# Second output projection: which heads its early part covers, and on which queue their rows are read

## Chip, cores and metric

The kernel runs on one core of one Trainium2 chip. The metric is the device time of one execution in microseconds. Beside the times there is a profile of one execution: the instructions of each engine with their start and duration, the DMA transfers, and what each engine waited for.

Engines: TensorE (PE; its weight loads are listed apart as PEld), VectorE (DVE), ScalarE (ACT), GpSimd (POOL) and SyncE (SP, which here only issues DMAs). Each engine has a stream of instructions of its own, and a DMA issue is an instruction in the stream of the engine that issues it.

## What is computed

A trunk of two layers over 1024 tokens of width 1024. Layer 0 mixes tokens by windowed attention, layer 1 by a bidirectional gated linear recurrence (HGRN2) of eight heads. Each mixer also has four cross-attention heads into 256 memory tokens. All twelve heads of 128 columns share one output projection, and a ConvGLU block follows. The part that matters is layer 1's mixer and its output projection:

```python
def mixer_hgrn2(u, mem_kv, w_in, lb_fwd, lb_bwd, norm_g, w_out):
    q, i, zf, zb, gate, xq = jnp.split(u @ w_in, [...], axis=-1)
    ...
    o = (gla_chunked(q, k_f, v, lf_f)
         + flip_t(gla_chunked(flip_t(q), flip_t(k_b), flip_t(v), flip_t(lf_b))))
    o = rmsnorm(o, norm_g.reshape(HG_HEADS, HG_VAL_DIM)).reshape(bsz, t, HG_W).astype(u.dtype)
    o = o * jax.nn.silu(gate)
    return jnp.concatenate([o, memory_cross_attn(xq, mem_kv)], axis=-1) @ w_out

    # in the trunk
        h = h + rmsnorm(y, norm_g[layer, 1])
        f = conv_ffn(rmsnorm(h, norm_g[layer, 2]), ...)
        h = h + rmsnorm(f, norm_g[layer, 3])
```

## The kernel before

**Precision.** Large products are made of three matmuls. An operand x is split into `h` (ACT casts it to fp32r) and `l` (DVE subtracts `h` from x). `mm3` (L81 to L83) then adds up h·h, h·l and l·h. So each operand costs an ACT instruction and a DVE instruction before PE may use it, and each weight unit (L75 DMA into a staging tile `st`, L76 cast, L77 subtraction) as well.

**Layer 1's mixer** (`hgrn`). Heads 0 to 7 run one after another. The normalised input lies transposed in `uh` and `ul`, eight blocks of 128 rows by 1024 tokens. A head is projected from it (matmuls into `pj`), then goes through four passes (two directions by two halves of 512 tokens), a long chain of small DVE, ACT and PE steps (`E`, `EP`, `ER`, `pa`, `pt`, `kT`, `pu`, `S`). At the end of the head, `output` makes `po`, normalises it (`on`, L1304), transposes it (`pt`, L1308) and, for heads 0 to 6, scales it into `ot` (L1316) and stores it from SP to the DRAM tensor `oT[1]` (L1317), one store for each half of the tokens, the upper half first. Head 7 isn't stored: its result is split straight into block 7 of `uh` and `ul` (L1312, L1313), whose input columns nobody needs any more. The projections of head 7 are spread over its passes: the last two are f for the upper half of the tokens (f1) and b for the lower half (b0). The cross-attention heads are fitted between the passes of the even heads and store their rows into blocks 8 to 11 of `oT[1]` from ACT (L224).

**The second output projection** (class `Out`, object `wo1`). It contracts the twelve blocks with weights in six units; unit u serves heads 2u and 2u+1. The output's 1024 columns are made in two halves of 512. The eight token tiles of 128 go in the order 4, 5, 6, 7, 0, 1, 2, 3. `groups` names which heads are contracted when, in the first half of the columns:

- `begin` (early part): for each tile, `read` brings the rows of `groups[0]`, here heads 0 to 6, from `oT[1]` into the place of the used-up `ul` (L536, on SP) and splits them (L537 on ACT, L538 on DVE); `kept` multiplies them into a PSUM bank `pb` (3 matmuls for each head); L569 copies the bank to `y0`. Two banks, which the projections used until then, are taken in turn. PE can do this while head 7 is still in its passes.
- `finish` (late part): for each tile, `cross` reads and multiplies the cross heads 8 to 11 (L551, L86, L87), `kept` adds `groups[2]`, here head 7, and L598 adds the early part's `y0`. Four more PSUM banks come with it.
- then, still in `finish`, the second half of the columns: all of heads 0 to 7 from `uh` and `ul`, then the cross heads again, then the residual, the norm and its transposition back into `uh` and `ul` for the ConvGLU block.

**Weight units.** `units` is the order in which they are loaded: the first four go to a ring of four slots as head 7's projection weights leave it (L76 and L77 with `wh`, `wl`), the last two to a pool of their own (`xwh`, `xwl`) whose memory is free only when head 7's passes are done. Before, the order is 0, 1, 2, 3, 4, 5.

**What sets the order.** Nobody writes the streams out by hand. A scheduler, which runs the program against its own estimates of durations, puts each instruction into the stream of its engine when it is ready and free by those estimates; among those that are ready the one earlier in the program goes first, and `tc.high_priority(AHEAD)` moves an instruction 2000 places ahead in that ranking. On the chip the streams then stand fixed. Before, layer 1's reads have no such priority (`self.order[:2 - 2 * self.l]` is empty for l = 1).

`Out` serves layer 1 alone; layer 0's projection has a class of its own, which the change leaves as it is.

Of the kernel before, what the change touches and what calls it, by code (L numbers as in the profile page):

```python
# [6 lines left out]
F32 = mybir.dt.float32  # L7
# [9 lines left out]
P = 128  # L17
# [29 lines left out]
def build(tc, A, out):  # L47
    nc = tc.nc
    act, dve, pool, pe = nc.scalar, nc.vector, nc.gpsimd, nc.tensor
# [3 lines left out]
    oT = [dram.tile([12, P, T], F32, name=f"oT{l}") for l in range(2)]  # L53
# [15 lines left out]
    def wunit(src, n=1024, pl=None, eng=None):  # L69

        tg = ("wh", "wl") if pl is None else ("xwh", "xwl")
        h = (pl or ring).tile([P, 1024], F32R, tag=tg[0], name=tg[0])
        l = (pl or ring).tile([P, 1024], F32R, tag=tg[1], name=tg[1])
        raw = stg.tile([P, 1024], F32, tag="st", name="st")[:, :n]
        nc.sync.dma_start(raw, src)  # L75
        act.copy(h[:, :n], raw)  # L76
        (eng or dve).tensor_tensor(l[:, :n], raw, h[:, :n].bitcast(F32), op=ALU.subtract)  # L77
        return h, l
# [10 lines left out]
    def rstd_of(pl, ss, n, count, tag):  # L89
        ms = pl.tile([P, n], F32, tag=tag + "ms", name=tag + "ms")  # L90
        dve.tensor_scalar(ms, ss, 1.0 / count, EPS, op0=ALU.mult, op1=ALU.add)
        rs = pl.tile([P, n], F32, tag=tag + "rs", name=tag + "rs")
        pool.tensor_tensor(rs, ms, nhalf[:, :n], op=ALU.pow)
        return rs

    def sumsq(pl, src, ss, j=None):
        n = src.shape[-1]
        if j is None:
            j = pl.tile([P, n], BF16, tag="junk", bufs=1, name="junk")
        act.activation(j[:, :n], src, AF.Square, accum_out=ss)  # L100

    def grow(pl, src_row, name):
        g = pl.tile([P, D], F32, tag=name, bufs=1, name=name)
        nc.sync.dma_start(g, src_row.to_broadcast([P, D]))
        return g
# [265 lines left out]
    class WOut:  # L371
# [3 lines left out]
        def __init__(self, l, src, key, order):  # L375
            self.l, self.src, self.key, self.order = l, src, key, order
            self.pools = [[], [], []]
            self.pre, self.part, self.begun, self.us = {}, {}, {}, {}
            self.psb, self.tag, self.psb2 = None, "pb", None
# [29 lines left out]
        def bank(self):  # L409
            if self.psb2:  # L410
                return self.psb2.tile([P, 512], F32, tag="pb2", name="pb")
            return self.psb.tile([P, 512], F32, tag=self.tag, name="pb")
# [99 lines left out]
    class Out:  # L512

        def __init__(self, l, src, key, order):
            self.l, self.src, self.key, self.order = l, src, key, order
            self.us, self.wf, self.banks, self.used = {}, None, [], 0
            n = (6, 7)[l]
            self.groups = (range(0, n), range(8, 12), range(n, 8))
            self.units = ((0, 1, 2, 4, 5, 3), (0, 1, 2, 3, 4, 5))[l]

        def bank(self):
            pl, tag = self.banks[self.used % len(self.banks)]
            self.used += 1
            return pl.tile([P, 512], F32, tag=tag, name="pb")

        def load(self, b, pl=None, n=6):
            for i, u in enumerate(self.units[:n]):
# [1 line left out]
                    self.us[b, u] = wunit(A[self.key][b, u], pl=pl if i >= RING else None)  # L529
            self.b = b  # L530

        def read(self, t):
            k = self.groups[0]
            c = (slice(None), slice(0, len(k)), slice(t * P, (t + 1) * P))
            raw = ul[c].bitcast(F32)
            nc.sync.dma_start(raw, oT[self.l][0:len(k), :, c[2]].rearrange("k p t -> p k t"))  # L536
            act.copy(uh[c], raw)  # L537
            dve.tensor_tensor(ul[c], raw, uh[c].bitcast(F32), op=ALU.subtract)  # L538

# [15 lines left out]
                c = slice((k % 2) * 512, (k % 2 + 1) * 512)  # L555
                mm3(ps, oh[:, i, :], ol[:, i, :], wh[:, c], wl[:, c], first and i == 0, last and i == 3)

        def begin(self, psb, tag, n, y0):
            self.psb, self.y0 = psb, y0
            self.banks += [(psb, tag)] * n  # L560
            for t in self.order:
                if t in self.order[:2 - 2 * self.l]:
                    with tc.high_priority(AHEAD):
                        self.read(t)
                else:
                    self.read(t)
                ps = self.bank()
                self.kept(ps, t, self.groups[0], True, True)
                act.copy(y0[t], ps)  # L569
            self.used = 0  # L570
# [11 lines left out]
        def finish(self):  # L582
            l = self.l
            self.wf = tc.alloc_tile_pool(name=f"wf{l}", bufs=1, side="right", reuse_waits="tile") if l == 0 else None
            wp = tc.alloc_tile_pool(name=f"wo{l}", bufs=2, side="right", reuse_waits="tile")
            psp = tc.alloc_tile_pool(name=f"wops{l}", bufs=2, space=PSUM, side="right", reuse_waits="tile")
            n = NT - 2 - len(self.banks)
            psb2 = tc.alloc_tile_pool(name=f"wopc{l}", bufs=n, space=PSUM, reuse_waits="tile")
            self.banks += [(psb2, "pb2")] * n
            y0 = self.y0  # L590
            s0 = wp.tile([P, NT], F32, bufs=1, name="s0")
            for t in self.order:
                ps = self.bank()
                self.cross(ps, t, True, False)
                self.kept(ps, t, self.groups[2], False, True)
                if t == self.order[5]:
                    after = self.last_read
                dve.tensor_tensor(y0[t], ps, y0[t], op=ALU.add)  # L598
                sumsq(wp, y0[t], s0[:, t:t + 1])
            with tc.issue_after(after.ins):  # L600
                g1 = grow(wp, A["norm_g"][l, 1:2, :], "g1")
                g2 = grow(wp, A["norm_g"][l, 2:3, :], "g2")
                xs = {}
                for t in self.order[:2]:
                    xs[t] = self.rows(wp, t)
            self.load(1, self.w1)
            self.first = wunit(A["ffw1"][l, 0, :, :1024], pl=self.wf) if l == 0 else None
            for t in self.order:
                pool.tensor_tensor(y0[t], y0[t], g1[:, :512], op=ALU.mult)
            for t in self.order:  # L610
                ts_ = slice(t * P, (t + 1) * P)
                ps = self.bank()
                self.kept(ps, t, range(8), True, False)
                self.cross(ps, t, False, True)
                x = xs[t] if t in xs else self.rows(wp, t)
                ss = wp.tile([P, 1], F32, tag="ss1", name="ss1")
                sumsq(wp, ps, ss)
                y1 = wp.tile([P, 512], F32, tag="y1", name="y1")
                dve.tensor_tensor(y1, ps, g1[:, 512:], op=ALU.mult)
                dve.tensor_tensor(ss, ss, s0[:, t:t + 1], op=ALU.add)  # L620
                rs = rstd_of(wp, ss, 1, D, "p")
                for c, y in ((slice(0, 512), y0[t]), (slice(512, 1024), y1)):
                    dve.scalar_tensor_tensor(x[:, c], y, rs[:, 0:1], x[:, c], op0=ALU.mult, op1=ALU.add)
                nc.sync.dma_start(h1d[l][ts_, :], x)
                norm_T(wp, psp, x, g2, uh, ul, t)
            psp.release()
            psb2.release()
            self.psb.release()
            wp.release()
            self.w1.release()  # L630
# [412 lines left out]
    def hgrn():  # L1043
        l = 1
# [7 lines left out]
        psj = tc.alloc_tile_pool(name="hgpj", bufs=2, space=PSUM, reuse_waits="tile")  # L1052
        PB = dict(pt=2, pu=1, po=1)

        def bank(tag, shape=(P, 4, P)):
            return psp.tile(list(shape), F32, tag=tag, bufs=PB[tag], name=tag)

        class Bank:
            tile = staticmethod(lambda shape, dt, tag, bufs, name: psp.tile(shape, dt, tag=tag, bufs=bufs, name=name))

        tags = {"pj": ("pj", 2, psj), "ps": ("pt", 2, Bank), "pt": ("pt", 2, Bank), "po": [lambda x=x: bank(x, (P, 512)) for x in ("po", "pu")], "sm": 1, "xo": "ot"}
        one = lambda shape, name, dt=F32: wp.tile(shape, dt, bufs=1, name=name)
        for x in PB:
            bank(x)
# [292 lines left out]
            if h < 7:  # L1357
                cur = proj(h + 1)
        free = [x[:, i].rearrange("p a b -> p (a b)") for i in (2, 0) for x in (V, G)]
        wo1.begin(psj, "pj", 2, {t: free[i // 2][:, (i % 2) * 512:(i % 2 + 1) * 512] for i, t in enumerate(wo1.order)})  # L1360
        psp.release()
        wp.release()
        return late
# [32 lines left out]
    wo1 = Out(1, h2d, "wout1", [4, 5, 6, 7, 0, 1, 2, 3])  # L1396
    start()
    window()
    wo0.finish()
    ffn(0, wo0, h2d, True, (0, 1), (0, 1))  # L1400
    late = hgrn()
    wo1.finish()
    late.release()
# [84 lines left out]
```

## Time and profile before

| | |
|---|---|
| time, median of 3 runs | 2695.96 us (2693.84 to 2696.16) |
| the profiled execution | 2697.36 us, of which the span is 2695.5 us |
| PE, PEld busy | 2622.5 us (97%), 2202.1 us (82%) |
| DVE, ACT, POOL busy | 1831.1 us (68%), 1385.1 us (51%), 468.2 us (17%) |
| early part: first split on ACT, last copy to `y0` | 1896.2 us, 1950.2 us |
| late part: first cross matmul | 1949.7 us |
| early reads L536, 8 of 448 KB | issued 1892.3 to 1903.1 us, 5.5 us to landing (median) |
| cross reads L551, 12 of 256 KB from 1880 to 1980 us | issued 1913.4 to 1976.4 us |

How to read it: times are microseconds from the start of the span. A line of the timeline is the start, the duration, engine, source line, operation, output<-inputs by the program's names, and in brackets how long the engine had idled before it and what it waited for. A line of the waits is "who <- whom: us in total, times, longest". The chain is followed back from the last instruction, at each step to what released it. The granted clock (PEclk) is TensorE's, as a share of full speed.

### The profile page before, as it was taken

The page shows a single profiled execution, that of the slowest core. Times are in us where ns is not written, and L with a number is a line of the kernel's source. Part 1 is how long each engine was busy: PE and PEld are TensorE (multiplying, and loading weights), DVE is VectorE, ACT ScalarE, POOL GpSimd, SP SyncE. Part 2 cuts the span into 40 slices and gives each one's busy share as a digit, 9 for nine tenths or more (in the row PEclk, how much of TensorE's full clock was granted, in tenths as well). Part 3 has the DMA queues.
Part 4 walks back from the last instruction along what each step waited for, and adds up shares of the span by engine and source line. Part 5 has one row for each costly group of instructions (what it writes and reads, how often), then busy time and mean ns, then how long its engine had stood idle before and what let it go on. Part 6 is the DMA issues. An engine that isn't in the chain of part 4 may idle for free.

```text
span 2695.5 us, 39322 instructions
## 1 busy us (share of the span) xinstructions
PE 2622.5 (97%) x14496; PEld 2202.1 (82%) x14496; DVE 1831.1 (68%) x3024; ACT 1385.1 (51%) x2528; POOL 468.2 (17%) x520
## 2 busy tenths in 40 slices
PE   8899999999999999999999999999899999999998
PEld 7888897788888887887887888888788788888887
DVE  6487777678655555478778686886657756556447
ACT  6367666645444445454455554555534444444443
POOL 1221110111111100032223141231121111110013
PEclk9899999999999999999999999999999999999999
DMA  7674213557877756574225252101446777775656
GB/s 281 209 163 108 59 28 115 178 181 181 217 196 203 200 168 244 190 243 149 102 98 160 77 128 60 48 29 63 120 166 164 198 198 205 197 203 159 224 193 233
DMA packets 205362, 427.00 MB, mean 158 GB/s; under 512 B 20080, under 2 KB 67568, under 8 KB 199536
## 3 DMA queue, kind: packets, MB, share of 16 engines
q1 hardware_dynamic: 178176, 329.83, 37.5%
q0 software_dynamic: 24544, 90.19, 16.1%
q10 hardware_dynamic: 2448, 4.46, 0.4%
q8 instruction: 114, 1.87, 0.3%
q14 instruction: 80, 0.66, 0.1%
HBM read 331.08 MB, written 117.44 MB: 166 GB/s over the span
## 4 chain that ended last, share of the span: by engine, by line
PE 76%; DVE 13%; ACT 4%; DMA 4%; issue 2%; POOL 1%; SPq 0%; DVEq 0%; POOLq 0%; ACTq 0%
PE X L639 26%; PE V L639 11%; PE pj L81 5%; PE pj L82 5%; PE Y L639 5%; PE pj L83 5%; PE pb L82 3%; PE pb L81 3%; PE pb L83 3%; DVE E L1195 1%; DVE ER L1230 1%; DVE wl L77 1%; PE pt L338 1%; DVE wl L87 1%; PE pt L116 1%
## 5 line engine op out<-in xcount | busy, mean ns | idle before, releaser
L87 DVE TENSOR_TENSOR wl<-st,wh 128x1024 fp32r<-128x1024 f32 (+1 forms) x238 | 263.5, 1114 | 324.7 <-ACT wh L86 303.1
L86 ACT CAST wh<-st 128x1024 fp32r<-128x1024 f32 (+1 forms) x238 | 222.5, 936 | 288.9 <-PE X L639 191.4
L81 PE MATMUL pj<-uh,wh 128*128 128x512 f32 x512 | 204.1, 399 | 4.9 <-DVE xl L87 2.5
L639 PE MATMUL X<-wl,wh 128*128 128x512 f32 x528 | 204.8, 390 | 0.3 <-DVE wl L87 0.3
L639 PE MATMUL X<-wh,wl 128*128 128x512 f32 x528 | 204.6, 389 | 0.0
L82 PE MATMUL pj<-ul,wh 128*128 128x512 f32 x512 | 202.8, 396 | 0.1
L83 PE MATMUL pj<-uh,wl 128*128 128x512 f32 x512 | 202.2, 395 | 0.0
L639 PE MATMUL X<-wh 128*128 128x512 f32 x528 | 198.8, 390 | 0.8 <-ACT c L1012 0.6
L81 PE MATMUL pj<-wh,uh 128*128 128x384 f32 (+1 forms) x512 | 191.0, 373 | 3.9 <-DVE gs L1126 3.9
L82 PE MATMUL pj<-wl,uh 128*128 128x384 f32 (+1 forms) x512 | 187.9, 367 | 0.0
L83 PE MATMUL pj<-wh,ul 128*128 128x384 f32 (+1 forms) x512 | 187.4, 367 | 0.0
L77 DVE TENSOR_TENSOR wl<-st,wh 128x1024 fp32r<-128x1024 f32 (+1 forms) x92 | 121.6, 1328 | 29.1 <-ACT wh L76 28.1
L639 PE MATMUL V<-uh,wh 128*128 128x512 f32 x344 | 133.8, 389 | 0.0
L639 PE MATMUL V<-ul,wh 128*128 128x512 f32 x344 | 133.8, 389 | 0.0
L639 PE MATMUL V<-uh,wl 128*128 128x512 f32 x344 | 133.8, 389 | 0.0
L76 ACT CAST wh<-st 128x1024 fp32r<-128x1024 f32 (+1 forms) x99 | 99.9, 1015 | 52.3 <-PE pj L82 30.2
L81 PEld LDWEIGHTS pj<-uh,wh 128*128 128x128 f32 x512 | 97.1, 190 | 25.4 <-DVE xl L87 2.9
L639 PEld LDWEIGHTS X<-wh 128*128 128x128 f32 x528 | 99.1, 188 | 22.2 <-ACT c L1012 1.0
L639 PEld LDWEIGHTS X<-wl,wh 128*128 128x128 f32 x528 | 99.1, 188 | 21.1 <-DVE wl L87 0.7
L639 PEld LDWEIGHTS X<-wh,wl 128*128 128x128 f32 x528 | 99.1, 188 | 20.5
L83 PEld LDWEIGHTS pj<-uh,wl 128*128 128x128 f32 x512 | 97.0, 189 | 19.2
L82 PEld LDWEIGHTS pj<-ul,wh 128*128 128x128 f32 x512 | 96.9, 189 | 18.8 <-DVE ul L87 0.4
(366 smaller groups left out, 7204.9 us busy)
## 6 DMA issues: line engine op xcount, KB each, us to landing
st<-hid SPq DMA_DIRECT2D x154, 256.0 KB, 3.1
st<-in_ffw_dram SPq DMA_DIRECT2D x108, 256.0 KB, 3.2
w2s<-in_ffw_dram POOLq DMA_DIRECT2D x24, 1024.0 KB, 7.8
st<-in_ffw_dram SPq DMA_DIRECT2D x46, 512.0 KB, 3.8
hid<-tt SPq DMA_DIRECT2D x88, 256.0 KB, 4.6
st<-w2s SPq DMA_DIRECT2D x88, 256.0 KB, 3.1
sx<-in_ffw_dram SPq DMA_DIRECT2D x84, 256.0 KB, 4.0
sy<-in_ffw_dram SPq DMA_DIRECT2D x42, 512.0 KB, 6.2
```

What stands on the lines that cost most here:

```text
L76: act.copy(h[:, :n], raw)
L77: (eng or dve).tensor_tensor(l[:, :n], raw, h[:, :n].bitcast(F32), op=ALU.subtract)
L81: pe.matmul(o, ah, bh, start=first, stop=False)
L82: pe.matmul(o, ah, bl, start=False, stop=False)
L83: pe.matmul(o, al, bh, start=False, stop=last)
L86: act.copy(h, src)
L87: dve.tensor_tensor(l, src, h.bitcast(F32), op=ALU.subtract)
L116: pe.transpose(ps[:, k, :], u[:, (4 * b + k) * P:(4 * b + k + 1) * P], ident)
L338: pe.transpose(tp[:, j, :], sm[:, j, c * P:(c + 1) * P], ident)
L639: pe.matmul(o, x, y, start=new, stop=e, skip_group_check=not first)
L1195: dve.tensor_tensor_scan(B[:, rev], smask, a_[:, rev], 0.0, op0=ALU.mult, op1=ALU.add)
L1230: dve.tensor_tensor(re_, re_, bc(pl_[:, :, e:e + 1], [P, nb, n]), op=ALU.mult)
```

## The change

The early part takes heads 0 to 5, and the late part heads 6 and 7. The early rows are read from ACT's queue instead of SP's; the reads and splits of the first two tiles (4 and 5) get the priority AHEAD. Head 6's rows are read apart, after the early part in the program, from SP's queue, in two transfers of 512 tokens, the upper half first. The load order of the weight units becomes 0, 1, 2, 4, 5, 3, so that the ring's fourth slot takes unit 4 (cross heads 8 and 9), and the separate pool takes units 5 and 3. The rewritten `bank` and `banks` name the number of buffers of each tag; for this kernel it stays two and four.

```diff
@@ class Out, __init__
-            n = (6, 7)[l]
-            self.groups = (range(0, n), range(8, 12), range(n, 8))
-            self.units = ((0, 1, 2, 4, 5, 3), (0, 1, 2, 3, 4, 5))[l]
+            self.groups = (range(0, 6), range(8, 12), range(6, 8))
+            self.units = (0, 1, 2, 4, 5, 3)
@@ bank
-            pl, tag = self.banks[self.used % len(self.banks)]
+            pl, tag, n = self.banks[self.used % len(self.banks)]
             self.used += 1
-            return pl.tile([P, 512], F32, tag=tag, name="pb")
+            return pl.tile([P, 512], F32, tag=tag, bufs=n, name="pb")
@@ read
-        def read(self, t):
-            k = self.groups[0]
-            c = (slice(None), slice(0, len(k)), slice(t * P, (t + 1) * P))
+        def read(self, ks, c0, c1, eng):
+            c = (slice(None), slice(ks[0], ks[-1] + 1), slice(c0, c1))
             raw = ul[c].bitcast(F32)
-            nc.sync.dma_start(raw, oT[self.l][0:len(k), :, c[2]].rearrange("k p t -> p k t"))
+            eng.dma_start(raw, oT[self.l][ks[0]:ks[-1] + 1, :, c0:c1].rearrange("k p t -> p k t"))
             act.copy(uh[c], raw)
             dve.tensor_tensor(ul[c], raw, uh[c].bitcast(F32), op=ALU.subtract)
@@ begin
-        def begin(self, psb, tag, n, y0):
+        def begin(self, psb, tags, y0):
             self.psb, self.y0 = psb, y0
-            self.banks += [(psb, tag)] * n
-            for t in self.order:
-                if t in self.order[:2 - 2 * self.l]:
+            self.banks += [(psb, t, tags.count(t)) for t in tags]
+            eng = (nc.sync, act)[self.l]
+            for i, t in enumerate(self.order):
+                if i < 2:
                     with tc.high_priority(AHEAD):
-                        self.read(t)
+                        self.read(self.groups[0], t * P, (t + 1) * P, eng)
                 else:
-                    self.read(t)
+                    self.read(self.groups[0], t * P, (t + 1) * P, eng)
@@ hgrn, its end
-        wo1.begin(psj, "pj", 2, {t: free[i // 2][...] for i, t in enumerate(wo1.order)})
+        wo1.begin(psj, ("pj",) * 2, {t: free[i // 2][...] for i, t in enumerate(wo1.order)})
+        for b in (1, 0):
+            wo1.read(range(6, 7), b * 512, (b + 1) * 512, nc.sync)
```

More of the change, by code (lines that the diff above doesn't have):

```diff
@@ L588, in finish @@
             psb2 = tc.alloc_tile_pool(name=f"wopc{l}", bufs=n, space=PSUM, reuse_waits="tile")
-            self.banks += [(psb2, "pb2")] * n
+            self.banks += [(psb2, "pb2", n)] * n
             y0 = self.y0
@@ L1359, in hgrn @@
         free = [x[:, i].rearrange("p a b -> p (a b)") for i in (2, 0) for x in (V, G)]
-        wo1.begin(psj, "pj", 2, {t: free[i // 2][:, (i % 2) * 512:(i % 2 + 1) * 512] for i, t in enumerate(wo1.order)})
+        wo1.begin(psj, ("pj",) * 2, {t: free[i // 2][:, (i % 2) * 512:(i % 2 + 1) * 512] for i, t in enumerate(wo1.order)})
+        for b in (1, 0):
+            wo1.read(range(6, 7), b * 512, (b + 1) * 512, nc.sync)
         psp.release()
```

## The prediction

> **What bounds the kernel now.** I read the page first, then the busy time of each engine in stretches around the change, the waits of TensorE there, and the chain that ended last.
>
> ```profile
> span 2695.5 us, 39322 instructions
> ...
> PE 2622.5 (97%) x14496; PEld 2202.1 (82%) x14496; DVE 1831.1 (68%) x3024; ACT 1385.1 (51%) x2528; POOL 468.2 (17%) x520
> ```
>
> TensorE (PE) has work in 97% of the span, so only a hole on PE can be won, and a hole filled early moves the end. The stretches:
>
> ```profile
> core 0: us, PE busy (x) PEld busy (x) DVE busy (x) ACT busy (x) POOL busy (x), PEclk, DMA share, GB/s
> 1883.60:1885.70 2.10, 2.04 (x69) 1.52 (x68) 2.10 (x6) 1.67 (x4) 0.65 (x3) 1.00 0.01 4
> 1885.70:1889.70 4.00, 0.00 (x0) 0.00 (x0) 3.97 (x6) 1.80 (x4) 1.01 (x1) 1.00 0.37 109
> 1889.70:1897.20 7.50, 3.58 (x16) 2.94 (x16) 6.15 (x14) 5.19 (x10) 1.53 (x2) 0.77 0.70 214
> 1897.20:1901.30 4.10, 4.08 (x73) 3.41 (x74) 4.09 (x7) 3.44 (x5) 1.01 (x2) 0.58 1.01 273
> 1901.30:1920.00 18.70, 18.37 (x152) 15.05 (x151) 17.62 (x29) 9.51 (x16) 5.83 (x6) 1.00 0.43 113
> 1920.00:1950.00 30.00, 30.00 (x162) 25.64 (x161) 13.03 (x25) 13.49 (x31) 4.17 (x4) 1.00 0.21 63
> ...
> 1977.00:2040.00 63.00, 63.00 (x300) 52.61 (x299) 38.71 (x64) 23.96 (x49) 9.65 (x14) 1.00 0.40 142
> ```
>
> Columns: the stretch, its length, then busy us of PE, weight loads, DVE, ACT, POOL, then the granted clock. From 1885.70 to 1901.30 PE idles 4.00 + 3.92 + 0.02 = 7.9 us. The last projection matmul of the eighth head (head 7):
>
> ```profile
> 1883.21 0.40 PE L83 MATMUL pj<-uh,wl 128*128 128x512 f32 x1
> ```
>
> The early part of the second output projection starts only at 1897.2. The waits in the hole, then the chain through it:
>
> ```profile
> PE pt L1269 <- ACT ot L1316: 4.1, 1, 4.1
> PE pb L81 <- ACT uh L537: 3.2, 1, 3.2
> ```
>
> ```profile
> 1889.08 0.60 ACT ot L1316
> 1889.69 2.55 DMA oT<-ot
> ...
> 1892.31 3.90 DMA ul<-oT
> 1896.23 0.95 ACT uh L537
> 1897.22 0.54 PE pb L81
> ```
>
> The early part reads heads 0 to 6 in one transfer, so it needs head 6 written: ACT makes `ot`, it lands 2.55 us later, only then is `ul` read (3.90), split (0.95), multiplied. Heads 0 to 5 had long been in DRAM.
>
> **The clock in the hole.** The rows give 0.77 and 0.58. At full clock the busy 3.58 and 4.08 us would have been 3.58 x 0.77 and 4.08 x 0.58, so 0.8 + 1.7 = 2.5 us are lost to it. The Trainium skill (TensorE: Matmul & The Clock Gate, "What's actually happening") says that an idle window of about 3.4 us halves the clock until about as long a busy one; one such window costs 1.7 us, an estimate from that page. The trace has a slow stretch of 11.6 us, longer than one such window, so the row stands; by the page the sum below would be 0.8 us smaller.
>
> The hole is thus worth 7.9 + 2.5 = **10.4 us** at most, plus 0.3 from 1901.30 to 1920.00 that I leave aside.
>
> **The change, part by part.**
>
> *Reads of heads 0 to 5 alone.* The wait for `ot` and its landing is gone. What remains is that the columns of `ul` and `uh` are free and the weights ready:
>
> ```profile
> 1874.84 0.68 DVE L1145 TENSOR_SCALAR s<-pj 128x512 f32<-128x512 f32 x1
> 1875.44 1.21 DVE L77 TENSOR_TENSOR wl<-st,wh 128x1024 fp32r<-128x1024 f32 x1
> ...
> 1885.15 0.69 DVE L1145 TENSOR_SCALAR s<-pj 128x512 f32<-128x512 f32 x1
> 1885.76 2.04 DVE L77 TENSOR_TENSOR wl<-st,wh 128x1024 fp32r<-128x1024 f32 x1
> ```
>
> The order of token tiles is 4, 5, 6, 7, then 0 to 3. Columns 512 and up (tiles 4 to 7) are last read by the projection that L1145 empties at 1874.84 (f1), columns below 512 by b0, emptied at 1885.15. The third weight unit, heads 4 and 5, is split by 1875.44 + 1.21 = 1876.65; only the fourth comes at 1887.8, and after the change that is the cross heads' unit, needed much later. So tiles 4 and 5 can be read from about 1875, land by 1879 (3.90) and be split before PE runs dry at 1885.7. PE then has two tiles at once, 2 x 18 matmuls. One matmul costs 0.228:
>
> ```profile
> 2050.18 5.48 PE X L639 x24
> ```
>
> so 36 x 0.228 = 8.2 us, and with the transposes and products of head 7 that ran in the hole (3.58 x 0.77 = 2.8) PE is fed to 1885.7 + 11.0 = 1896.7.
>
> *First two splits ahead.* They come before head 7's chain on ACT and DVE. The durations, grouped by shape:
>
> ```profile
> L538 DVE TENSOR_TENSOR ul<-ul,uh 128x896 fp32r<-128x896 f32 x8 | 8.9, 1116 | 1.8 <-ACT uh L537 1.8
> L537 ACT CAST uh<-ul 128x896 fp32r<-128x896 f32 x8 | 7.5, 942 | 4.5 <-DMA ul<-oT 4.4
> ...
> L87 DVE TENSOR_TENSOR ol<-ol,oh 128x512 fp32r<-128x512 f32 x5 | 3.3, 685 | 6.1 <-ACT oh L86 6.1
> ...
> L86 ACT CAST oh<-ol 128x512 fp32r<-128x512 f32 x5 | 3.1, 621 | 4.9 <-DMA ol<-oT 3.0 <-PE pb L82 1.9
> ```
>
> For 768 columns, between 512 and 896: DVE 0.685 + 2/3 x 0.431 = 0.97, ACT 0.84. All ten splits (eight of 768, two of 512) cost DVE 8 x 0.97 + 2 x 0.69 = 9.1 against 8.9, ACT 7.9 against 7.5: +0.2 and +0.4 us. Two pulled ahead put 1.9 us of DVE before head 7's chain.
>
> ```profile
> 1870.00:1921.00 51.00, 42.67 (x389) 35.24 (x388) 47.87 (x86) 29.86 (x56) 14.48 (x15) 0.93 0.40 114
> ```
>
> DVE is busy 47.87 of 51 us there and spares only 3.1; ACT spares 21.1. So DVE is full, and the third tile's split, which is not ahead, gets its turn late. Before, the first split found its place on DVE at 1897.2, after a gap that shows how the chain ahead of it ebbs:
>
> ```profile
> 1897.20 1.09 DVE L538 TENSOR_TENSOR ul<-ul,uh 128x896 fp32r<-128x896 f32 x1 [1.03 <-ACT uh L537]
> ```
>
> PE runs dry at 1896.7; with the subtraction after it that is a pause between 0 (splits squeezed in earlier) and 3 us. I take **1.5**.
>
> *ScalarE's queue.* Eight issues leave SP and go to ACT, in whose stream an instruction holds up all behind it. The bounds of one issue: the stores that ACT issues already, and SP's own issues of these rows:
>
> ```profile
> L224 ACTq DMA_DIRECT2D oT<-xo x16: 326/326/343, 213.4 to 1884.9; - x16
> ```
>
> ```profile
> 1892.31 3.23 SPq L536 DMA_DIRECT2D ul<-oT  x4
> ...
> 1901.46 3.50 SPq L536 DMA_DIRECT2D ul<-oT  x4
> ```
>
> So 8 x 0.33 = 2.6 us below, and (3.23 + 3.50) x 6/7 = 5.8 above. The second is the same access, so I take 5.8; ACT's 21.1 us of spare time hide it, unless it falls in head 7's exponentials that DVE waits for. Nothing for the sum, 0 to 2 for the range. In exchange SP's queue no longer holds reads behind stores:
>
> ```profile
> SPq L536 <- DMA oT<-ot: 6.6, 2, 4.4
> ```
>
> The Trainium skill (DMA: Bandwidth & Descriptors, "Issuing engines are not separate DMA queues") speaks against this part: another issuing engine saves its issue time, not transfer time. By that rule the queue alone would gain at most the 6.7 us of SP's issues, none of them on PE's path; what the row above shows is an ordering wait of 6.6 us on SP, and that is what goes.
>
> *Head 6's rows later.* Two reads of 256 KB on SP, after head 6's stores; behind them wait the cross heads' reads, of which the first goes out at 1913.4:
>
> ```profile
> L551 SPq DMA_DIRECT2D ol<-oT x12: 360/371/507, 1913.4 to 1976.4; - x12
> ```
>
> That is 12 us after the last of head 6's stores had landed (1901.46 in the row of SP above), so nothing is delayed. The 24 matmuls (8 x 3) of head 6 move to the late part, 24 x 0.228 = 5.5 us moved, not saved.
>
> *Order of weight units.* In the second half unit 3 is split last, as it was already:
>
> ```profile
> 1983.09 2.32 DVE L77 TENSOR_TENSOR wl<-st,wh 128x1024 fp32r<-128x1024 f32 x1
> ```
>
> It ends at 1985.4. PE does two tiles' first six heads, 36 matmuls or 8.2 us, before it needs it, and the second half begins near 1977:
>
> ```profile
> 1985.07 0.39 PE L83 MATMUL pb<-wh,ul 128*128 128x512 f32 x1
> ```
>
> So it is needed at 1985.1 to 1985.4. There is no slack, so a microsecond later is a microsecond lost; a microsecond earlier wins nothing. Its slot comes free at the same matmul as before. I take 0, -0 to +2.
>
> *The tail of head 7.* PE reaches the end of the early part sooner, by 10.4 and by the 5.5 moved:
>
> ```profile
> 1938.82 1.13 DVE L1304 SCALAR_TENSOR_TENSOR on<-po,ors,gs 128x128 f32<-128x128 f32 x4 [1.19 <-POOL ors L93]
> ...
> 1944.48 0.75 DVE L1313 SCALAR_TENSOR_TENSOR ul<-pt,bng,uh 128x512 fp32r<-128x512 f32 x1 [4.53 <-ACT uh L1312]
> ```
>
> ```profile
> 1949.71 0.62 PE L81 MATMUL pb<-xwh,oh 128*128 128x512 f32 x2
> ```
>
> Before, head 7's rows were ready at 1945.2, 4.5 us ahead of PE's first late matmul at 1949.7. After, PE is there at 1949.7 - 10.4 - 5.5 = 1933.8 and has the cross heads of two tiles without new banks (24 x 0.228 = 5.5, to 1939.3), of six with all banks (16.4, to 1950.2). Head 7's chain has slack too: its `on` was done at 1939.95 and its subtraction ended 5.3 us later, 4.5 of which DVE idled for a transpose whose turn on PE had not come and the copy behind it. Shortfall 0 to 5.9; I take 0, for that reason.
>
> **Sum**, against the profiled execution (2697.36 us, of which 2695.5 are the span): 10.4 - 1.5 = 8.9, so 2688.5. The median shown, 2695.96, lies 1.4 below that execution: **2687.1 us**. Its own range is gains of 6 to 12, 2684 to 2690.
>
> **Rivals.**
>
> *The transposes keep their place.* PE's order is fixed beforehand. If the transposes that wait for `ot` (4.1) stand ahead of the new products, that wait stays with 1 us of clock: gain 8.9 - 5.1 = 3.8, 2692.2. For it: the wait is the longer one in the hole, and its cause, DVE's 2.04 us split at 1885.76, is still there. Against: from 1901 on products and transposes alternate with 0.3 us of PE idle.
>
> *The two tiles aren't early.* If the reads wait for b0 as well, they go out at 1883.6 and PE starts at 1883.6 + 3.9 + 1.0 = 1888.5, 2.8 us idle with 0.5 of clock: gain 5.6, 2690.4. For: `ul` is one tile. Against: the eight subtractions into it were made one tile after another while PE multiplied the tiles before them, with 0.3 us of PE idle from 1901.30.
>
> *ACT is held, slower than before.* A read of tiles 0 to 3 that stands early in ACT's stream waits there for b0's end, with head 7's exponentials behind it. The row that shows the kind:
>
> ```profile
> 1882.94 1.05 ACT L76 CAST wh<-st 128x1024 fp32r<-128x1024 f32 x1 [2.06 <-PE pj L82]
> ```
>
> From 1877 to 1883.6 that is 6.6 us; with 5.8 of issues and 1.9 of splits head 7's end goes from 1945.2 to 1959.5. PE, out of work at 1939.3 or 1950.2, idles 20 or 9 us and loses 2.5 of clock: 12 or 1 us slower net; 2703 in the middle. It decides from the point where head 7's end passes 1949.7 (1939.3 + 10.4), 4.5 us late. For: DVE spares 3.1 us only, so nothing is caught up. Against: ACT idles in the places where the reads become ready, and the 2.06 us quoted here is the longest hold of ACT by PE's projections in that place.
>
> **How the numbers follow.** Forecast 0.62, transposes 0.14, not early 0.08, ACT held 0.16. About 0.2% (5.4 us) can be told from no change: faster is under 2690.6, slower over 2701.4. From the cases: faster 0.60 + 0.04 + 0.04 = 0.68; slower 0.14; the rest, 0.18, the same. The range 2683 to 2700 leaves out most of the slower case and a little below.
>
> **What would show it.** Right: PE's wait for L537 gone; reads of tiles 4 and 5 on ACT's queue at 1875 to 1880; the clock at 1.00 through 1901; PE busy over 14 of the 15.6 us. Pause: a PE wait for the third tile's split near 1896. Wrong: a PE wait for L1312 or L1313 near 1940, a long hold on ACT before a read, or a new PE wait on unit 3 near the start of the second half.

## The result and the profile after

The changed kernel takes 2689.75 us (median of 15 runs, 2686.47 to 2694.8) beside 2696.09 for the kernel before in the same comparison (15 runs): a ratio of 0.9974, 95% interval 0.9967 to 0.9981, or 5.1 to 8.9 us gained and 6.3 between the medians. The profiled execution took 2686.47 us. Its span and busy times:

```profile
span 2684.7 us, 39333 instructions
...
PE 2618.3 (98%) x14496; PEld 2200.0 (82%) x14496; DVE 1827.6 (68%) x3026; ACT 1384.6 (52%) x2530; POOL 469.4 (17%) x520
```

Lines after the changed ones have moved by one: L1269 of before is L1268, L1304 is L1303, and so on; the early reads, casts and subtractions are L534, L535 and L536.

**Where to measure.** The spans differ by 10.8 us, more than the change can be credited with: this execution was already 3.56 us ahead before the first instruction that differs. So I measure a stage. It begins at the second of head 7's four clips `s<-pj` (the instruction that empties a projection's PSUM bank; the third is f1's, the fourth b0's), up to which both programs are the same, and ends at the start of the last `y<-pb` of the second output projection. In the timeline of VectorE, before:

```profile
1867.46 0.69 DVE L1145 TENSOR_SCALAR s<-pj 128x512 f32<-128x512 f32 x1 [0.51 <-PE pj L83]
...
2050.02 0.69 DVE L619 TENSOR_TENSOR y<-pb,g 128x512 f32<-128x512 f32 x1
```

and after:

```profile
1863.90 0.69 DVE L1144 TENSOR_SCALAR s<-pj 128x512 f32<-128x512 f32 x1 [0.51 <-PE pj L83]
...
2038.04 0.68 DVE L618 TENSOR_TENSOR y<-pb,g 128x512 f32<-128x512 f32 x1
```

That is 182.56 and 174.14 us: the stage is 8.4 us shorter. The same stage in stretches, before:

```profile
1867.46:1910.00 42.54, 34.54 (x288) 28.48 (x286) 38.11 (x66) 27.41 (x55) 12.12 (x12) 0.92 0.46 130
1910.00:1960.00 50.00, 49.67 (x312) 41.80 (x311) 26.42 (x50) 20.50 (x45) 6.68 (x7) 1.00 0.27 84
```

and after:

```profile
1863.90:1910.00 46.10, 45.17 (x349) 38.02 (x348) 40.24 (x72) 31.16 (x64) 14.20 (x12) 1.00 0.40 121
1910.00:1960.00 50.00, 47.75 (x305) 40.13 (x303) 28.93 (x55) 22.40 (x53) 14.39 (x13) 1.00 0.45 147
```

Up to 1910, PE's idle time falls from 8.0 to 0.93 us and the clock rises from 0.92 to 1.00. From 1910 to 1960 it rises from 0.33 to 2.25 us: part of the gain is given back there. PE's waits from 1860 to 2100 after the change name both remainders:

```profile
PE pt L1307 <- DVE on L1303: 2.3, 1, 2.3
PE X L638 <- DVE u7l L87: 1.7, 1, 1.7
PE pt L116 <- DVE nu L112: 1.4, 1, 1.4
PE pt L1268 <- ACT ot L1315: 0.9, 1, 0.9
PE Y L638 <- DVE wl L87: 0.5, 1, 0.5
```

The wait for `uh` is gone, of the 4.1 us for `ot` 0.9 is left, and the 2.3 us for `on` is new; the others come after the early part, and the kernel before has them too. ACT's queue shows when the rows were read:

```profile
1868.68 1.57 ACTq L534 DMA_DIRECT2D ul<-oT  x3
1870.74 0.93 ACTq L534 DMA_DIRECT2D ul<-oT  x1
1878.56 0.37 ACTq L534 DMA_DIRECT2D ul<-oT  x1
1878.97 1.15 ACTq L534 DMA_DIRECT2D ul<-oT  x2
1880.23 1.01 ACTq L534 DMA_DIRECT2D ul<-oT  x1
```

Four tiles' reads, not two, are out by 1871.7, and their subtractions on VectorE follow, done by 1880.7; PE's early products start at 1879.16 and never wait for one of them:

```profile
1874.75 2.92 DVE L536 TENSOR_TENSOR ul<-ul,uh 128x768 fp32r<-128x768 f32 x2
1878.87 1.81 DVE L536 TENSOR_TENSOR ul<-ul,uh 128x768 fp32r<-128x768 f32 x2
1884.78 2.69 DVE L536 TENSOR_TENSOR ul<-ul,uh 128x768 fp32r<-128x768 f32 x3
1888.33 0.95 DVE L536 TENSOR_TENSOR ul<-ul,uh 128x768 fp32r<-128x768 f32 x1
```

**The new hole**, in PE's timeline:

```profile
1925.88 0.40 PE L81 MATMUL pb<-wh,oh 128*128 128x512 f32 x1
...
1933.13 0.39 PE L1297 MATMUL po<-v,As 128*128 128x128 f32 x2
...
1936.52 0.63 PE L83 MATMUL pb<-xwh,ul 128*128 128x512 f32 x2
1939.40 1.01 PE L1307 MATMUL pt<-ident,on 128*128 128x128 f32 x4 [2.25 <-DVE on L1303]
1940.17 0.48 PE L81 MATMUL pb<-wh,oh 128*128 128x512 f32 x1
```

PE multiplies the cross heads of two tiles from 1925.88, then head 7's last output (`po`, 1933.13), six products, and then it stands before the transposes of that output. The third tile's first product (1940.17) comes only behind them.

### The profile page after: what moved, and what is told of

The parts are those of the page before. It is cut to its first block, busy times and chain, and to the rows that moved or that the text cites. A ratio compares the mean times of both kernels' runs of the same rounds, so it can differ in the third digit from the quotient of the medians.

```text
span 2684.7 us, 39333 instructions
## 1 busy us (share of the span) xinstructions
PE 2618.3 (98%) x14496; PEld 2200.0 (82%) x14496; DVE 1827.6 (68%) x3026; ACT 1384.6 (52%) x2530; POOL 469.4 (17%) x520
## 4 chain that ended last, share of the span: by engine, by line
PE 77%; DVE 13%; ACT 4%; DMA 3%; issue 2%; POOL 1%; SPq 0%; DVEq 0%; ACTq 0%; POOLq 0%
PE X L638 27%; PE V L638 11%; PE pj L81 5%; PE pj L82 5%; PE Y L638 5%; PE pj L83 5%; PE pb L82 3%; PE pb L81 3%; PE pb L83 3%; DVE E L1194 1%; DVE ER L1229 1%; PE pt L338 1%; PE pt L116 1%; DVE wl L87 1%; PE po L1297 1%
## 5 line engine op out<-in xcount | busy, mean ns | idle before, releaser
L980 POOL TENSOR_TENSOR c<-c,g 128x512 f32<-128x512 f32 x24 | 43.4, 1828 | 393.8 <-PE X L638 162.8
```

The source lines that it names most:

```text
L980: pool.tensor_tensor(y[q][:, t, :], y[q][:, t, :], g3[:, c], op=ALU.mult)
```

## The experiments

The stage is measured as above in each kernel; the third column is its length, the fourth the waits of PE in it that differ, and the granted clock where it fell below 1.00 (from 1940 to 1960; in the fourth row from 1890 to 1910).

| kernel | ratio to before, 95% interval | stage, us | waits and clock |
|---|---|---|---|
| changed kernel | 0.9974 (0.9967 to 0.9981) | 174.14 | on 2.3, ot 0.9 |
| again | 0.9975 (0.9966 to 0.9984) | 175.68 | on 2.3, ot 1.2, clock 0.91 |
| a third time | 0.9974 (0.9962 to 0.9985) | 176.42 | on 2.3, ot 1.1, gs 0.7, clock 0.91 |
| seven heads early, rest kept | 0.9998 (0.9990 to 1.0007) | 183.05 | ot 4.1, uh 3.1, clock 0.64 and 0.67 |
| six heads, queue and priority as before | 0.9982 (0.9973 to 0.9990) | 178.15 | on 2.3, ul 1.6, ot 0.2, clock 0.83 |
| change with SyncE's queue | 0.9977 (0.9967 to 0.9988) | 174.23 | on 2.3, ot 1.1 |
| last output of head 7 ahead | 0.9988 (0.9980 to 0.9997) | 180.3 | five waits, 1.0 to 1.6 each, clock 0.91 |
| second half's weights later | 0.9985 (0.9976 to 0.9994) | 179.05 | on 4.6, ot 0.5, gs 0.5, clock 0.83 |
| six heads, other banks | 1.0000 (0.9992 to 1.0009) | 174.87 | on 2.3, gs 0.6, uh 0.4, ot 0.2; behind the stage nu 7.5 |
| third tile first, right banks | 1.0010 (1.0002 to 1.0019) | 172.34 | ot 1.2, gs 0.5; behind the stage nu 8.1 |
| third tile first, left banks | 0.9960 (0.9948 to 0.9972) | 171.33 | ot 0.9 |
| the same again | 0.9954 (0.9940 to 0.9968) | 172.84 | ot 1.5, gs 0.7 |
| the same, SyncE's queue, no priority | 0.9970 (0.9958 to 0.9982) | 170.66 | ot 0.3 |

Where the last output was put ahead, the first mark itself was moved; so its length is taken from the next clip (172.88 us to the last `y`, against 166.76 in the changed kernel: 6.1 longer, hence 180.3). Where one run is set against another here, a difference in the ratio under about 0.001 (some 3 us) can't be told from none; the stage is one execution's, and among the three of the changed kernel it varies by 2.3 us.

**Which part of the change gains?** First the six heads and the order of weight units that goes with them taken back, queue and priority kept:

```diff
-            self.groups = (range(0, 6), range(8, 12), range(6, 8))
-            self.units = (0, 1, 2, 4, 5, 3)
+            self.groups = (range(0, 7), range(8, 12), range(7, 8))
+            self.units = (0, 1, 2, 3, 4, 5)
@@ hgrn, its end
-        for b in (1, 0):
-            wo1.read(range(6, 7), b * 512, (b + 1) * 512, nc.sync)
```

> The other half alone: heads 0 to 6 as before, with the unit order of before, but read from ACT's queue with the first two tiles ahead. Theory (the wait for head 6's rows is what counts): the hole stays, PE idles 7 us or more between the last projection and the first early product, stage 181 to 186, and ACT, whose stream now holds the reads that wait for head 6's stores, is held 2 us or more at a time: median 2695 to 2700. Rival (queue and priority make the gain): stage 176 or less, median 2690.

Its waits are those of before:

```profile
PE pt L1268 <- ACT ot L1315: 4.1, 1, 4.1
PE pb L81 <- ACT uh L535: 3.1, 1, 3.1
...
PE pu L1273 <- ACT kT L1270: 0.7, 1, 0.7
```

Nothing is gained (0.9998): without the six heads, queue and priority do nothing. Then the other way about, the six heads alone:

```diff
-            eng = (nc.sync, act)[self.l]
+            eng = nc.sync
             for i, t in enumerate(self.order):
-                if i < 2:
+                if i < 0:
```

> Only the heads are changed: the early part takes heads 0 to 5, head 6's rows come later, but all reads stay on SP's queue and no tile is put ahead. Compared by the length of the stage from head 7's second-last-but-one L1144 (the last instruction that stands alike in all streams) to the last L618: 182.6 us before (1867.46 to 2050.0), 174.1 after (1863.9 to 2038.0). Theory (the wait for head 6's rows was the whole hole): PE has no wait for the early split, stage 174 to 176, median 2689 to 2691. Rival (queue and priority make the gain): SP's reads stay behind stores or DVE splits too late, a PE wait of 3 us or more for the split or for ot, stage 179 to 183, median 2694 to 2696.

The early part is as good as in the change (`uh` never waited for, `ot` 0.2 us), but the stage is 4.0 us longer than in the changed kernel's first trace, 178.15, which lies between the two cases expected. The tail shows why:

```profile
1939.09 1.01 PE L1307 MATMUL pt<-ident,on 128*128 128x128 f32 x4 [2.25 <-DVE on L1303]
1941.66 0.79 PE L81 MATMUL pb<-wh,oh 128*128 128x512 f32 x1 [1.56 <-DVE ul L1312]
...
1947.38 0.63 PE L82 MATMUL pb<-xwl,uh 128*128 128x512 f32 x1
```

In the tail the order of PE is that of the change, but the third tile's first product waits for `ul`, the last reader of the transposes' result, which it does not use. In the compiled program the reason is a PSUM bank (pools on the right take the highest free banks, pools on the left the lowest):

```
                                        last transposes   third tile   norms' transposes   ConvGLU's sums
changed kernel                          bank 3            bank 2       6, 7                0 to 5
six heads, queue and priority as before bank 2            bank 2       6, 7                0 to 5
change with SyncE's queue               bank 3            bank 2       6, 7                0 to 5
six heads, other banks                  bank 2            bank 6       4, 5                0 to 5
third tile first, right banks           bank 3            bank 6       4, 5                0 to 5
third tile first, left banks            bank 5            bank 2       6, 7                0 to 5
last output of head 7 ahead             bank 2            bank 2       6, 7                0 to 5
```

`pt` has two banks and takes the one that comes free first; with the reads on SyncE's queue and no tile ahead, two copies on ACT changed places (`ot` ahead of `kT`), and from there on the two banks are exchanged. So the third tile's sum stands in the bank that `ul` and `uh` of head 7 still read. Beside its 1.56 us, the matmuls behind both waits took 0.63 us instead of 0.39 until 1947.8, 20 x (1 - 0.83) = 3.4 us of clock:

```profile
1940.00:1960.00 20.00, 18.44 (x69) 14.91 (x69) 4.91 (x7) 6.43 (x15) 6.38 (x5) 0.83 0.26 89
```

1.6 + 3.4, less the 0.7 that this order saves at `ot`, is 4.3 for the 4.0 us. That is against the changed kernel's best trace; against its other two, whose clock fell as well, the stage is 2.5 and 1.7 us longer, and the ratios (0.9982 and 0.9974) are some 2 us apart, with intervals that overlap. So the loss is 2 to 4 us. Two runs tested its cause: the change with its reads on SyncE's queue (where no bank collides) and the six heads alone with the third tile's sum in another bank. The first:

```diff
-            eng = (nc.sync, act)[self.l]
+            eng = nc.sync
```

> The change with its reads on SyncE's queue, as before, and everything else kept (six heads, first two tiles ahead). The third tile's PSUM bank is here not the one that the last transposes of head 7 write. Theory that the bank of the third tile made the loss of the run with heads alone: no wait of pb for ul in the tail, clock 1.00 from 1940 to 1960, stage 173.5 to 174.5 us, ratio within 0.0007 of the changed kernel's. Rival, that ScalarE's queue is what the change needs: stage 177 to 179 us, 4 us behind the changed kernel.

> The changed kernel once more, on the chip of the runs beside it, as their measure. Stage length (from the second-last of the clips s<-pj of head 7 to the last y) 174.1 us as in its first trace if that trace is typical; ratio to the kernel before 0.9974. If its first trace was a lucky one, another length, 175 to 178.

0.9977 beside 0.9975 on one chip, and stages of 174.23 beside 174.14 and 175.68: no gain of the queue can be seen. The Trainium skill (DMA: Bandwidth & Descriptors, "Issuing engines are not separate DMA queues") says that ACT and SP share the same DMA engines and that another issuing engine saves no transfer time; these two runs agree. What the priority adds by itself was not run: without it, with ACT's queue, the compiled program has the same order of instructions on every engine.

The second, six heads alone with other banks:

```diff
+psa = tc.alloc_tile_pool(name="wopa", bufs=2, space=PSUM, side="right", reuse_waits="tile") if l else None
+self.banks += [(psa, "pa2", 2)] * 2 * l
 psp = tc.alloc_tile_pool(name=f"wops{l}", bufs=2, space=PSUM, side="right", reuse_waits="tile")
 n = NT - 2 - len(self.banks)
```

> The run with heads alone (reads on SyncE's queue, no tile ahead) with one more edit: the third and fourth tiles' sums stand in the two PSUM banks that the heads' score sums had, so that none of them is the bank of the last transposes. Bank theory: the 1.6 us wait of pb for ul is gone and with it the drop of the clock to 0.83, so the stage falls from 178.2 to 173.5 to 174.5 us, and the time by 3 to 4.5 us against the run with heads alone. Rival, that the reads' queue or order made the loss: stage stays at 177 to 179 us.

Through the stage every engine's order is that of the six heads alone. The wait for `ul` is gone, the clock 1.00, the stage 174.87 for 178.15: the bank was the cause of the wait. How much of the clock it took with it is less sure, since the wait for `on` alone lowers the clock in some executions (last section). Yet the time, expected to fall, rose to that of before (1.0000), by a wait behind the stage that nobody had forecast:

```profile
PE pt L116 <- DVE nu L112: 8.9, 2, 7.5
```

The norms' transposes had moved to banks 4 and 5, which ConvGLU's sums use; so no product of ConvGLU could stand ahead of the last of them, and PE idled 7.5 us. From the stage's end to the end of the span it took 653.4 us, against 645.5 in the kernel before, which uses up the stage's gain. In the changed kernel PE's order has 49 of ConvGLU's products ahead of the last tile's transposes, and these find their rows ready.

**What holds the tail?** The 2.3 us for `on` stay in all of these. Two simple remedies did not help. The first gave head 7's output the priority AHEAD:

```diff
-                output(h, r, b, qin, S, As)
+                with tc.high_priority(AHEAD if h == 7 else 0):
+                    output(h, r, b, qin, S, As)
```

> The changed kernel with head 7's output steps put ahead by the same priority. In the changed kernel PE waits 2.25 us for head 7's on (L1303) while cross products are still to be done. Theory (the order on PE and DVE makes this wait: po was ready at 1929.8 but had its turn at 1933.1): the wait falls under 0.5, stage 172. Rival (the chain of states itself is too late): the wait stays above 1.5, stage 174 or more.

```profile
PE pb L81 <- DVE ul L1312: 1.6, 1, 1.6
PE pu L1273 <- DVE S L1282: 1.5, 1, 1.5
PE pt L1307 <- DVE on L1303: 1.5, 1, 1.5
...
PE pb L83 <- DVE ol L87: 1.0, 1, 1.0
PE pb L81 <- ACT uh L1311: 1.0, 1, 1.0
```

The wait for `on` falls only to 1.5, and the chain of head 7 stalls PE at five places instead of one. One of them, the 1.6 us for `ul`, is the bank again: in this program too the two banks are exchanged (last row of the table of banks), so the run does not test the priority alone. Without that 1.6 us and the clock (20 x 0.09 = 1.8 us) the stage would still be 2.7 us longer than the changed kernel's first, an estimate from these numbers. The second took the second half's weights, three of whose splits (1.22 us each on DVE) stand in the tail, behind the read of the fifth tile:

```diff
+                if t == self.order[4]:
+                    later = self.last_read
...
-            self.load(1, self.w1)
+            with tc.issue_after(later.ins):
+                self.load(1, self.w1)
```

> The changed kernel with the weight units of the second half of the columns read only after the cross rows of the fifth tile. Theory (three weight subtractions of 1.22 us stand between head 7's last state steps on DVE, 1924.8 to 1929.4, and hold the chain back): the state steps end 2.5 to 3.7 us earlier and PE's wait of 2.25 for on falls to 0.5 or less, stage 172. Rival (PE's own order sets it): the wait stays, stage 174; and if the units are then late for the second half, PE waits there for a weight, stage 175 to 178.

The wait doubles to 4.6 us. On DVE and ACT the splits now fall between `po` and `on`; DVE's line of two of them and of what came behind:

```profile
1942.79 2.50 DVE L77 TENSOR_TENSOR wl<-st,wh 128x1024 fp32r<-128x1024 f32 x2
1945.20 1.28 DVE L599 TENSOR_TENSOR v<-pb,v 128x512 f32<-128x512 f32 x2
...
1947.75 1.13 DVE L1306 SCALAR_TENSOR_TENSOR on<-po,ors,gs 128x128 f32<-128x128 f32 x4 [1.19 <-POOL ors L93]
```

This suggests that the hole is not made by one slow step of the chain: PE lacks work between `po` and the transposes. The work exists (the third tile), but its bank is released only with head 7's pool. The next kernel keeps the two banks of the score sums (`pa`), idle by then, in a pool of their own and gives them to the third and fourth tile (the pool's release is left out here):

```diff
+        psa = tc.alloc_tile_pool(name="hgpa", bufs=1, space=PSUM, side="right", reuse_waits="tile")
         psp = tc.alloc_tile_pool(name="hgps", bufs=1, space=PSUM, side="right", reuse_waits="tile")
-        PA = [psp.tile([P, 4, P], F32, tag=f"pa{d}", bufs=1, name="pa") for d in range(2)]
+        PA = [psa.tile([P, 4, P], F32, tag=f"pa{d}", bufs=1, name="pa") for d in range(2)]
...
+        wo1.psa = psa
+        wo1.banks += [(psa, f"pa{d}", 1) for d in range(2)]
```

> The changed kernel with the two PSUM banks of the heads' score sums kept in a pool of their own, from which the third and the fourth tile of the second output projection take theirs; so PE's order has the third tile's products before the last output of head 7 and the fourth tile's between it and its transposes (39 products of 0.23 us, 8.9 us, where there were 6). Theory that the rest of the loss in the tail is this one hole: pt<-on wait under 0.3 us instead of 2.3, stage 174.1 - 2.3 = 171.5 to 172.5 us, ratio 0.9965. Rival, that the late head turns into a later wait of the products on its rows (uh, ul of head 7) or of the next tile's splits: a new wait of 1 to 3 us on ul or ol after the transposes, stage 173 to 176.

The stage came out as expected (172.34, no wait for `on`), and again the norms' banks (4 and 5) cost a wait of 8.1 us behind it, for 1.0010 in all. The stage is 10.2 us shorter than before and the rest of the span behind it 9.7 longer (655.1 for 645.5), which would leave the time as it was; the 3 us that the median is above it stay open. With `psa` on the left side, next to the projections' two banks, the norms' transposes are back in banks 6 and 7:

> As the run with the third tile before the last output, but the two kept PSUM banks lie next to the projections' two, so that the two banks of the norms' transposes are again outside the six that ConvGLU takes. Theory that both wider runs lost only by ConvGLU's first products having to wait for those transposes (waits of 7.5 and 8.1 us of pt for nu): one such wait of 1 to 1.5 us is left, as in the changed kernel, no pt<-on wait over 0.3 us, stage 171.5 to 173 us, time 1.5 to 3.5 us below the changed kernel's, ratio 0.9962 to 0.9970. Rival, that the second half's products pulled forward are what starved the end: a wait of 5 us or more of pt for nu stays, ratio 1.000.

```profile
PE X L640 <- DVE u7l L87: 1.7, 1, 1.7
PE pt L1271 <- ACT ot L1318: 0.9, 1, 0.9
PE pt L116 <- DVE nu L112: 0.8, 1, 0.8
PE Y L640 <- ACT wh L86: 0.6, 1, 0.6
```

In PE's timeline the last output and its transposes now stand 6.2 us apart, with products between them and no idle time:

```profile
1942.87 0.61 PE L1300 MATMUL po<-S,qin 128*128 128x128 f32 x4
1943.23 0.47 PE L83 MATMUL pb<-xwh,ul 128*128 128x512 f32 x1
...
1949.68 0.60 PE L1310 MATMUL pt<-ident,on 128*128 128x128 f32 x4
```

2686.12 us, a ratio of 0.9960. Two more runs were made beside each other, and one with SyncE's queue and no priority:

> The changed kernel a third time, beside the run with the third tile ahead and its banks left, on one chip: ratio 0.9975, stage 174 to 176 us, one wait of 2.3 us of pt for on.

> The run with the third tile ahead and its banks left once more. If its 0.996 was real: ratio 0.9955 to 0.9967, 2 to 4.5 us below the changed kernel beside it, stage 171 to 172 us and no pt<-on wait. If it was the chip's luck: ratio 0.9972 or more.

> The same with the reads on SyncE's queue and no tile ahead, so of the change only the six heads are left. If queue and tiles ahead are worth nothing: ratio within 0.0007 of the run beside it, stage within 1 us, 171.5 to 173 us. If they are worth something: 2 us or more behind it.

On one chip the changed kernel took 2691.6 us and this one 2686.59; ratios 0.9974 and 0.9954, whose intervals still overlap a little (0.9962 to 0.9985, 0.9940 to 0.9968), with stages of 176.42 and 172.84. So it is faster than the kernel before in both comparisons, and than the changed one by 5 us between the medians; the stage bears this out. Without queue and priority the stage is 0.7 to 2.2 us shorter still (170.66, `ot` 0.3), but the time is 2.0 us longer than beside it on one chip (2688.08 and 2686.12). The intervals overlap (0.9958 to 0.9982, 0.9948 to 0.9972), so whether queue and priority are worth anything here stays open.

## Why the prediction was right, and where its sum was off

**Direction and place: right.** 2687.1 was forecast, 2689.75 came, inside the likeliest case's own range (2684 to 2690), though at its slow end. The early part's hole closed by the reads that no longer wait for `ot`.

**The hole, 7.9 us idle.** It was there and is filled but for 0.9 to 1.2 us of `ot`. That is what is left of the first rival: the transposes that wait for `ot` did not stay ahead, but stand in PE's order behind 29 of the early products (1879.16 to 1888), and the rest of the wait is what these don't cover.

**The clock, 2.5 us.** Undersized. PE's busy time in the stage fell from 172.86 to 169.59 us, 3.3 us for the same products, and the row of before gives 42.54 x (1 - 0.92) = 3.4. The Trainium skill (TensorE: Matmul & The Clock Gate, "What's actually happening") would have it smaller: one window of about 3.4 us at half clock is 1.7 us, an estimate from that page; the runs side with the rows.

**The pause for the third tile, 1.5 us.** It did not come. Two steps failed. The first is the start of the reads: I put them behind the projections' clip, about 1875. But they overwrite blocks 0 to 5 only, which PE leaves before it comes to blocks 6 and 7. By the time of this execution, 3.56 us ahead, 1875 means 1871.4, and the first three reads went out at 1868.68, 2.8 us earlier. The second is that VectorE, being full, would come to the third tile late: it split the third and fourth tile from 1878.87 to 1880.68, ahead of steps of head 7. That did not make head 7 late: its last subtraction ended at 1941.92, and in before at 1945.23, which is 1941.67 by the time of this execution. The early start also disposes of the second rival, that the reads wait for b0.

**ScalarE's queue, 0 of a cost up to 2 us.** Right: its eight issues took 5.0 us, between the bounds 2.6 and 5.8, and with SyncE's queue no other time can be told (0.9977 beside 0.9975). The third rival, ACT held so long that head 7 is late, did not occur: between its reads ACT idled at most 1.73 us at a time, for VectorE, and all eight were out by 1881.3.

**Head 6's rows and the order of the weight units, 0.** Right: PE waits for neither.

**The tail of head 7, 0 of a shortfall up to 5.9 us.** This term failed. "Head 7's chain has slack too", I wrote, since `on` had lain finished in before. But its output `po` moves with PE: it stands behind the products of two tiles (1933.13), and from there the sum of squares, the square root and `on` take until 1939.40. I had counted that PE then has "the cross heads of two tiles without new banks"; these lay ahead of `po`, not behind it. The shortfall is 2.3 us of wait, and 1.2 to 1.8 us of clock with it in two of three executions (20 x 0.09 = 1.8 by the granted clock of 0.91; by PE's busy time in the stage 170.83 - 169.59 = 1.2). The kernel that puts the third and fourth tile there has no wait for `on`, and a stage 2.8 us (174.14 - 171.33) to 3.6 us (176.42 - 172.84) shorter than the changed kernel's, which shows the term; 0.6 of either comes from another place, the wait for `nu` (1.4 to 0.8).

**The sum**, against the first trace. PE's busy time in the whole stage, before and after:

```profile
sum 182.56, PE 172.86 PEld 144.07 DVE 119.70 ACT 84.90 POOL 38.06; mean PE 43.22 PEld 36.02 DVE 29.92 ACT 21.23 POOL 9.52
```

```profile
sum 174.14, PE 169.59 PEld 142.04 DVE 117.28 ACT 84.86 POOL 39.71; mean PE 42.40 PEld 35.51 DVE 29.32 ACT 21.21 POOL 9.93
```

Idle time fell from 9.70 to 4.55 us, 5.15, and busy time by 3.27, together 8.4 against 8.9. Errors cancelled, which is luck: +1.5 for the pause, +0.8 for the clock and +0.3 of idle time that I had left aside, against -2.3 for `on` and -0.9 for `ot`. That trace was the best of three; by the other two the stage is 6.9 and 6.1 us shorter than before, and this is what the medians show, 6.3.

## What to carry to other kernels

A read that needs the newest piece of its data together with old ones waits for the newest; split by age, it goes out when its target is free, and here that alone (with the order of weight units that goes with it) made the gain, on either queue. Before a hole is filled by moving work forward, look at what the chain behind it has then to hide behind: moved work leaves the place where it used to be cover. And where accumulators come from pools that are released and allocated again, look at which PSUM bank each stage takes: the order of two transposes and the side on which a pool lay were worth 2 to 4 and 8 us, where the whole change was worth 6.

## What was not expected of the hardware

The clock drops after shorter idle times than I had allowed for, and not every time. The same wait of 2.25 us before the same transposes left the clock at 1.00 in the changed kernel's first trace, and in its second and third it fell to 0.91 (in the run with SyncE's queue and in that with other banks, the same wait of 2.3 us left it at 1.00). PE's timeline in the second, from 1946.63:

```profile
1946.63 1.16 PE L1307 MATMUL pt<-ident,on 128*128 128x128 f32 x4 [2.25 <-DVE on L1303]
1947.44 0.77 PE L81 MATMUL pb<-wh,oh 128*128 128x512 f32 x1
1948.02 0.63 PE L82 MATMUL pb<-wl,oh 128*128 128x512 f32 x1
...
1950.15 0.52 PE L81 MATMUL pb<-xwh,oh 128*128 128x512 f32 x1
```

Matmuls of 0.63 us, one each 0.43, for 0.39 and 0.23: a little over half speed, for 3.5 us. The Trainium skill (TensorE: Matmul & The Clock Gate, "What's actually happening") lets the clock fall after an idle window of about 3.4 us that runs freely; that executions of one program differ agrees with the free running, but an idle time of 2.25 us, shorter than the window, was enough here. With a second wait of 1.56 us behind the first, in the run with six heads alone, the slow stretch was 6.1 us long. So this wait costs 2.3 us in one execution and up to 4 in another (2.3 and 1.2 to 1.8 of clock), and by the clock alone two executions of one program differ by more than 1 us in this stage.
